# A buffer of their own and an earlier issue for the adaLN weight parts, with three raw weight buffers in place of four

## The chip, the core and the metric

One core of a Trainium2 chip runs the whole network in one launch. The metric is the device time of one execution in microseconds (us). Lower is better.

## The reference

The network maps a sequence of 256 tokens of width 1024 (fp32) to one of the same shape. It has two blocks:

- The first block has four layers. Each is a gated FFN, an attention (differential, MoBA, NSA, differential again) and a second gated FFN, each with an RMS norm ahead and a residual sum behind.
- The second block has two layers. Each is a mixer (retention and causal pooling) and a gated FFN, and both are modulated by adaLN: shifts, scales and gates are computed from a vector c.

An FFN has 2816 hidden columns:

```python
def swiglu(x, w_in, w_out):
    gate, up = jnp.split(x @ w_in, 2, axis=-1)
    return (jax.nn.silu(gate) * up) @ w_out
```

The modulation of the second block is a product of one row with a matrix of 1024 x 6144 for each of the two layers:

```python
for l in range(DEPTH_2):
    mod = c_act @ w_ada[l] + b_ada[l]
    sh1, sc1, g1, sh2, sc2, g2 = jnp.split(mod, N_MOD, axis=-1)
    h = modulate(rmsnorm(x, norm1[l]), sh1, sc1)
    ...
    x = x + g1[:, None, :] * (merged @ w_out[l])
    h2 = modulate(rmsnorm(x, norm2[l]), sh2, sc2)
    gate, up = jnp.split(h2 @ w_ffn_in[l], 2, axis=-1)
    x = x + g2[:, None, :] * ((jax.nn.silu(gate) * up) @ w_ffn_out[l])
```

The modulation does not depend on x, so it can be computed at any time before the second block needs it.

## The kernel before

**Stages.** The network is cut into 16 stages. Stages 0, 2, 3, 5, 6, 8, 9 and 11 are the FFNs of the first block, and 1, 4, 7 and 10 its attentions. Stages 12 and 14 are the mixers of the second block and 13 and 15 its FFNs. Each stage opens a memory pool `mp` of its own, and an attention or mixer stage also `ap`. A pool `wp` for weights lives through the whole program.

**Weights.** Every weight is loaded from HBM in pieces of 1 MB into a buffer with the tag `raw` in `wp`. There are four of them (RAW_BUFS = 4): loads in `weights` (L182) and, for some pieces of `seven`, L447. ScalarE casts a piece in halves of 1024 columns to a high part (`hilo`, L171, into `hi`), VectorE subtracts it for the low part (L172, into `lo`). There are seven buffers of either kind (W_BUFS = 7). TensorE multiplies high by high, low by high and high by low (L220, L222 and L224). Once both halves are split, the raw buffer is free.

**An FFN** has 11 chunks of 256 hidden columns for each of two halves of the tokens. `f1` makes the first product of a chunk; `hidden` applies the gate on ScalarE (L414) and VectorE (L416, L417), whose result `hd` is transposed to `hT`; `f2` multiplies it with w_out and sums in PSUM (`aA`, `aB`). PLAN cuts the middle of the FFN into two units. A unit has two plain chunks and one pair of chunks that is computed with seven block products in place of eight (`seven`). Its operands are sums of quarters of w_in, made by transfers that accumulate (POOL, L452) into tiles `rs`, and sums and differences of quarters of x, which `halves_of_x` makes once in each FFN. It uses one raw buffer as scratch (tag `raw`), and writes the results `Sh` and `Sl` (L171 and L172).

**The order of the work** in a unit is a string, `"fo777fo7fo7fo7ooo7no"` (L542): f is a first product, o a second product, 7 a step of `seven`, n starts the next unit's loads. After its places 9 and 15 `ada_step` is called, in all stages but the first. The framework then schedules the instructions onto each engine's queue ahead of time, by program order and by when it thinks that operands are ready, and each engine runs its queue in order. Buffers with the same tag are handed out in program order.

**adaLN parts.** The scales and shifts of the second block are computed in the FFNs of stages 2, 3, 5, 6, 8, 9, 11 and 13, one vector of 1024 for each FFN, in four parts (u = 0 to 3). `ada_add` (L1173) loads 1 MB of w_ada into a raw buffer (SP, L1179) and adds its rows, scaled by c, to an accumulator with four VectorE instructions (L1185 or L1187). After the fourth part `ada_columns` sums over the partitions with two small products. Stage 15 has no `ada_step` work left, and stage 0 has none. The two gates of each second-block layer are computed the same way, by `start_gate` in stages 12 to 15: four parts, with `yield GATE_STEP` ahead of each `ada_add`.

Of the kernel before, what the change touches and what calls it, by code (L numbers as in the profile page):

```python
# [18 lines left out]
P = 128  # L19
D = 1024  # L20
# [13 lines left out]
POOL_WINDOWS = (2, 4, 8, 16)  # L34
UW = 1024

RAW_BUFS = 4
W_BUFS = 7
PREP_0 = 4.4
PREP_1 = 0.6  # L40
# [62 lines left out]
class _Net:  # L103
# [70 lines left out]
    def weights(self, srcs, a, b):  # L174


        raw = self.t(self.wp, [P, 2 * UW], "raw", bufs=RAW_BUFS)
        rv = raw[:, : a * b].rearrange("p (a b) -> p a b", a=a)
# [221 lines left out]
    def ffn(self, w_in, w_out, factors, finish, middle, scaled):  # L400


        nc = self.nc
        hT, wi, wo, acc = {}, {}, {}, {}
# [29 lines left out]
        def seven(c):  # L434
# [7 lines left out]
            def load(k, n, alone=False):  # L442
                if alone:
                    r = self.t(self.wp, [P, 2 * UW], "raw", bufs=RAW_BUFS).rearrange("p (a b) -> p a b", a=4)
                else:
# [73 lines left out]
            yield  # L519

        queue, sums = [], {}

        def pop():
            c, t = queue.pop(0)
            f2(c, t=t)

        first = ((0, 0), (0, 1), (1, 0), (1, 1)) if self.stage == 0 else ((0, 0), (1, 0), (0, 1), (1, 1))
# [40 lines left out]
    def halves_of_x(self, res, scaled):  # L568
# [15 lines left out]

        f = self.t(self.wp, [P, 2 * UW], "raw", bufs=RAW_BUFS).rearrange("p (a b) -> p a b", a=4)
        x = {}
# [267 lines left out]
    def compress(self, k2, w1, pe):  # L854
# [11 lines left out]
        for u in range(2):  # L866
            raw = self.t(self.wp, [P, 2 * UW], "raw", bufs=RAW_BUFS)
            rv = raw.rearrange("p (a b) -> p a b", a=8)
# [301 lines left out]
        self.oner = self.t(self.cp, [P, P], "oner", F32R)  # L1170
        nc.vector.tensor_scalar(self.oner, self.ident, 0.0, 1.0, op0=ALU.mult, op1=ALU.add)

    def ada_add(self, acc, l, i, u, first=False):  # L1173

        nc = self.nc
        src = self.cols(self.a["w_ada_2"][l], i * D, D, 2 * u, 2)
        raw = self.t(self.wp, [P, 2 * UW], "raw", bufs=RAW_BUFS)
        rv = raw.rearrange("p (a b) -> p a b", a=2)
        nc.sync.dma_start(rv, src)  # L1179
        for k in range(2):  # L1180
            c = self.ccol[:, 2 * u + k : 2 * u + k + 1]
            for q in range(2):
                r = slice(512 * q, 512 * q + 512)
                if first and k == 0:
                    nc.vector.tensor_scalar(acc[:, r], rv[:, k, r], c, None, op0=ALU.mult)  # L1185
                else:
                    nc.vector.scalar_tensor_tensor(acc[:, r], rv[:, k, r], c, acc[:, r], op0=ALU.mult, op1=ALU.add)  # L1187
# [16 lines left out]
    def ada_step(self):  # L1204

        if not self.ada_steps:
            return
        l, i, u = self.ada_steps.pop(0)
        if u == 0:
            self.ada_acc = self.t(self.mp, [P, D], "ada", bufs=1)  # L1210
        self.ada_add(self.ada_acc, l, i, u, u == 0)
        if u == 3:
            self.start(self.ada_columns(self.ada_acc, l, i))

    def ada_columns(self, acc, l, i):
        nc = self.nc
        o = (l * 6 + i) * KT
        m = self.mod[:, o : o + KT]
        sums = yield from self.over_partitions(acc)
        for q, ps in enumerate(sums):  # L1220
            tmp = self.t(self.fp, [P, 4, P], "res", bufs=2)
            nc.vector.tensor_tensor(tmp, ps.rearrange("p (a b) -> p a b", a=4),
                                    self.ident[:, None, :].to_broadcast([P, 4, P]), op=ALU.mult)
            nc.vector.reduce_sum(m[:, 4 * q : 4 * q + 4], tmp, axis=AX.X)
        nc.vector.tensor_tensor(m, m, self.bcol[:, o : o + KT], op=ALU.add)
# [4 lines left out]
    def start_gate(self, l, i):  # L1230


        nc = self.nc
        g = self.t(self.fp, [P, D], "gbc", bufs=1)
        self.gate_done = False

        def gen():
            yield 4.0
            nc.gpsimd.memset(g, 0.0)
            nc.gpsimd.dma_start(g[0:1], self.a["b_ada_2"][l : l + 1, i * D : i * D + D])  # L1240
            for u in range(4):
                yield GATE_STEP
                self.ada_add(g, l, i, u)
            yield 4.0
            sums = yield from self.over_partitions(g)
            for q, ps in enumerate(sums):
                nc.scalar.activation(g[:, 512 * q : 512 * q + 512], ps, AF.Copy, scale=0.5)
            self.gate_done = True

        self.start(gen())  # L1250
        return g
# [362 lines left out]
```

## Time and profile before

| | us |
|---|---|
| median of 3 runs | 2959.21 |
| lowest and highest | 2957.91 and 2966.21 |
| profiled execution, its own time | 2968.85 |
| its span, first to last instruction | 2967.1 |
| TensorE (PE) busy | 2849.1 (96%) |
| VectorE (DVE) busy | 2177.2 (73%) |
| ScalarE (ACT) busy | 1679.8 (57%) |
| GpSimd (POOL) busy | 432.9 (15%) |
| TensorE's mean granted clock | 0.989 |

The rows that the prediction reads come from one profiled execution. PE is TensorE's matmuls and PEld its weight loads. DVE is VectorE, ACT is ScalarE, SP is the engine whose queue issues most transfers. A row `B <- A: x, n, y` of a list of waits says that B was held up by A for x us in total, n times, y us at the longest. In a timeline, a bracket `[x <-A]` at the end of a row means that the engine stood idle for x us before this instruction and that A ended the idle time. A timeline row with `xN` joins N equal neighbours; its duration covers them all. The granted clock 1.00 is 2.4 GHz, 0.50 is 1.2 GHz.

### The profile page before, as it was taken

To read this page: it belongs to the slowest core of one execution; us is meant where nothing else is said; L and a number is where in the kernel's file an instruction comes from. 1 tells how busy PE (TensorE), PEld (TensorE's weight loads), DVE (VectorE), ACT (ScalarE), POOL (GpSimd) and SP (SyncE) were. 2 spreads that over 40 slices of the span, in tenths; PEclk is the share of its full clock that TensorE was granted. 3 is DMA by queue.
4 is the path that set the end of the run, shared out by engine and by line. 5 is a ranking of instruction groups with operands and counts; after the bars stand their busy time and mean duration, and the time that the engine had idled before them with its cause. 6 is when DMAs were issued, how large, how long until landed. Compare 5 with 4: busy or idle time off the path is not lost.

```text
span 2967.1 us, 36810 instructions
## 1 busy us (share of the span) xinstructions
PE 2849.1 (96%) x13165; PEld 2274.3 (77%) x13165; DVE 2177.2 (73%) x3275; ACT 1679.8 (57%) x2873; POOL 432.9 (15%) x601
## 2 busy tenths in 40 slices
PE   8999999999999999999999999999999999999998
PEld 6787777777777777778777777777778777788777
DVE  7665778877467787756777877677876688865776
ACT  6556655655665565556655555665554454644554
POOL 1112211111111021121111111211111101100110
PEclk9999999999999999999999999999999999999999
DMA  9864497796449779751698795459764679664694
GB/s 274 233 198 158 136 306 225 216 273 213 149 141 291 226 225 259 218 190 44 185 267 250 233 264 184 142 179 262 233 226 172 191 235 297 226 220 163 213 274 147
DMA packets 358043, 633.27 MB, mean 213 GB/s; under 512 B 15170, under 2 KB 190132, under 8 KB 357860
## 3 DMA queue, kind: packets, MB, share of 16 engines
q1 hardware_dynamic: 312724, 541.99, 53.7%
q0 software_dynamic: 44768, 88.30, 16.2%
q8 instruction: 104, 1.70, 0.2%
q14 instruction: 79, 0.65, 0.1%
q10 hardware_dynamic: 368, 0.62, 0.1%
HBM read 629.82 MB, written 1.05 MB: 213 GB/s over the span
## 4 chain that ended last, share of the span: by engine, by line
PE 68%; DVE 13%; DMA 8%; ACT 5%; issue 4%; POOL 2%; DVEq 0%; SPq 0%; ACTq 0%; POOLq 0%
PE mm L222 13%; PE mm L224 13%; PE mm L220 13%; DMA raw<-in_w_ada_dram 6%; DVE lo L172 5%; PE tp L252 4%; PE aA L222 4%; PE aA L224 4%; PE aA L220 4%; ACT hi L171 3%; PE aB L222 3%; PE aB L220 3%; PE aB L224 3%; DVE Sl L172 1%; DVE ada L1187 1%
## 5 line engine op out<-in xcount | busy, mean ns | idle before, releaser
L172 DVE TENSOR_TENSOR lo<-raw,hi 128x1024 fp32r<-128x1024 f32 x834 | 1005.2, 1222 | 294.0 <-ACT hi L171 286.9
L171 ACT CAST hi<-raw 128x1024 fp32r<-128x1024 f32 x834 | 865.9, 1051 | 371.3 <-PE mm L224 176.6
L220 PE MATMUL mm<-hi,xh 128*128 128x512 f32 (+2 forms) x1856 | 750.8, 406 | 39.6 <-DVE hd L417 33.0
L222 PE MATMUL mm<-lo,xh 128*128 128x512 f32 (+2 forms) x1856 | 735.7, 397 | 4.8 <-DVE lo L172 4.8
L224 PE MATMUL mm<-hi,xl 128*128 128x512 f32 (+2 forms) x1856 | 732.1, 395 | 2.4 <-DVE xl L172 1.4
L220 PEld LDWEIGHTS mm<-hi,xh 128*128 128x128 f32 x1856 | 352.6, 190 | 123.7 <-issue 31.6
L224 PEld LDWEIGHTS mm<-hi,xl 128*128 128x128 f32 x1856 | 353.2, 190 | 80.0 <-DVE xl L355 4.8
L222 PEld LDWEIGHTS mm<-lo,xh 128*128 128x128 f32 x1856 | 353.9, 191 | 78.1 <-DVE lo L172 14.7
L452 POOL DMA_DIRECT2D rs<-in_ffn_w_in_dram x128 | 157.2, 1300 | 1104.1 <-DVE lo L172 785.5
L171 ACT CAST hi<-rs 128x1024 fp32r<-128x1024 f32 x200 | 205.8, 1049 | 167.1 <-PE mm L224 155.4
L172 DVE TENSOR_TENSOR lo<-rs,hi 128x1024 fp32r<-128x1024 f32 x200 | 239.6, 1221 | 42.7 <-ACT hi L171 41.8
L222 PE MATMUL mm<-lo,Sh 128*128 128x512 f32 x560 | 227.2, 406 | 7.7 <-DVE lo L172 7.3
L220 PE MATMUL mm<-hi,Sh 128*128 128x512 f32 x560 | 226.8, 405 | 4.0 <-ACT hi L171 4.0
L224 PE MATMUL mm<-hi,Sl 128*128 128x512 f32 x560 | 221.2, 395 | 0.0
L220 PE MATMUL aB<-hi,hT 128*128 128x512 f32 x568 | 195.1, 402 | 10.4 <-ACT hT L264 10.4
L220 PE MATMUL aA<-hi,hT 128*128 128x512 f32 x584 | 198.9, 404 | 0.9 <-DVE s L661 0.9
L224 PE MATMUL aB<-hi,hT 128*128 128x512 f32 x568 | 192.2, 392 | 0.9 <-DVE hT L268 0.8
L222 PE MATMUL aA<-lo,hT 128*128 128x512 f32 x584 | 192.3, 392 | 0.0
L224 PE MATMUL aA<-hi,hT 128*128 128x512 f32 x584 | 191.8, 392 | 0.0
L222 PE MATMUL aB<-lo,hT 128*128 128x512 f32 x568 | 189.4, 393 | 0.0
L264 ACT CAST hT<-tp 128x256 fp32r<-128x256 f32 x268 | 94.7, 372 | 161.7 <-PE tp L252 161.5
L265 DVE TENSOR_TENSOR hT<-tp,hT 128x256 fp32r<-128x256 f32 x268 | 108.5, 420 | 68.2 <-ACT hT L264 67.7
(281 smaller groups left out, 3670.7 us busy)
## 6 DMA issues: line engine op xcount, KB each, us to landing
raw<-in_ffn_w_in_dram SPq DMA_DIRECT2D x224, 512.0 KB, 7.2
raw<-in_ffn_w_out_dram SPq DMA_DIRECT2D x88, 1024.0 KB, 5.7
rs<-in_ffn_w_in_dram POOLq DMA_DIRECT2D x128, 512.0 KB, 8.9
raw<-in_w_ada_dram SPq DMA_DIRECT2D x48, 1024.0 KB, 6.8
raw<-in_w_in_dram SPq DMA_DIRECT2D x44, 1024.0 KB, 5.2
rs<-in_ffn_w_in_dram SPq DMA_DIRECT2D x32, 1024.0 KB, 6.7
raw<-in_ffn_w_in_dram SPq DMA_DIRECT2D x32, 1024.0 KB, 8.6
raw<-in_w_ffn_in_dram SPq DMA_DIRECT2D x56, 512.0 KB, 5.1
```

Of the source, the lines that this page charges most:

```text
L171: self.nc.scalar.copy(hi, raw)
L172: self.nc.vector.tensor_tensor(lo, raw, hi.bitcast(F32), op=ALU.subtract)
L220: mm(ps, xh[k], wh[:, c], start=first, stop=False)
L222: mm(ps, xh[k], wl[:, c], start=False, stop=False)
L224: mm(ps, xl[k], wh[:, c], start=False, stop=last)
L252: self.nc.tensor.transpose(dst, src, self.ident[:k, :k])
L264: nc.scalar.copy(hi, v)
L265: nc.vector.tensor_tensor(lo, v, hi.bitcast(F32), op=ALU.subtract)
L452: nc.gpsimd.dma_start(r[:, 2 * q : 2 * q + 2], quarter(k, n)[:, 2 * q : 2 * q + 2], accum_op=ALU.add)
L1187: nc.vector.scalar_tensor_tensor(acc[:, r], rv[:, k, r], c, acc[:, r], op0=ALU.mult, op1=ALU.add)
```

## The change

- `ada_load` is split off from `ada_add`. In an FFN stage it loads a part into a tile `araw` in the stage's own pool `mp` (one buffer of the size of a raw one); in a mixer stage, into a raw buffer as before.
- `ffn` issues the load of part 0 at its start. `ada_step` adds the part that was loaded before and then issues the load of the next part, if the FFN has one more.
- In `start_gate` the load of a part stands ahead of `yield GATE_STEP` rather than behind it.
- RAW_BUFS is 3 in place of 4.

```diff
-RAW_BUFS = 4
+RAW_BUFS = 3
...
         queue, sums = [], {}
+        if self.stage > 0 and self.ada_steps:
+            self.ada_next = self.ada_load(*self.ada_steps[0])
...
-    def ada_add(self, acc, l, i, u, first=False):
-
-        nc = self.nc
+    def ada_load(self, l, i, u):
+
         src = self.cols(self.a["w_ada_2"][l], i * D, D, 2 * u, 2)
-        raw = self.t(self.wp, [P, 2 * UW], "raw", bufs=RAW_BUFS)
+        if self.stages[self.stage]["attention"]:
+            raw = self.t(self.wp, [P, 2 * UW], "raw", bufs=RAW_BUFS)
+        else:
+            raw = self.t(self.mp, [P, 2 * UW], "araw", bufs=1)
         rv = raw.rearrange("p (a b) -> p a b", a=2)
-        nc.sync.dma_start(rv, src)
+        self.nc.sync.dma_start(rv, src)
+        return rv
+
+    def ada_add(self, acc, rv, u, first=False):
+
+        nc = self.nc
...
-        self.ada_add(self.ada_acc, l, i, u, u == 0)
+        self.ada_add(self.ada_acc, self.ada_next, u, u == 0)
         if u == 3:
             self.start(self.ada_columns(self.ada_acc, l, i))
+        else:
+            self.ada_next = self.ada_load(*self.ada_steps[0])
...
             for u in range(4):
+                rv = self.ada_load(l, i, u)
                 yield GATE_STEP
-                self.ada_add(g, l, i, u)
+                self.ada_add(g, rv, u)
```

## Rows read from the trace of the kernel before

**Rows 1.** The page: busy time, share of the span and instructions of each engine.
```profile
PE 2849.1 (96%) x13165; PEld 2274.3 (77%) x13165; DVE 2177.2 (73%) x3275; ACT 1679.8 (57%) x2873; POOL 432.9 (15%) x601
```
**Rows 2.** The page: the chain that ended last, by engine and line.
```profile
PE mm L222 13%; PE mm L224 13%; PE mm L220 13%; DMA raw<-in_w_ada_dram 6%; DVE lo L172 5%; PE tp L252 4%; PE aA L222 4%; PE aA L224 4%; PE aA L220 4%; ACT hi L171 3%; PE aB L222 3%; PE aB L220 3%; PE aB L224 3%; DVE Sl L172 1%; DVE ada L1187 1%
```
**Rows 3.** Waits of TensorE: total us, times, longest us.
```profile
PE mm L220 <- DVE hd L417: 33.0, 18, 4.3
```
**Rows 4.** Timeline of SP in stage 2: start us, us, queue, line, operation.
```profile
384.90 0.37 SPq L1179 DMA_DIRECT2D raw<-in_w_ada_dram  x1
...
395.89 0.37 SPq L1179 DMA_DIRECT2D raw<-in_w_ada_dram  x1
...
401.54 9.21 SPq L182 DMA_DIRECT2D raw<-in_ffn_w_in_dram  x4
```
**Rows 5.** Timeline of VectorE in the same stretch of stage 2.
```profile
390.85 0.48 DVE L1185 TENSOR_SCALAR ada<-raw,col 128x512 f32<-128x512 f32 x1
...
406.73 2.08 DVE L1187 SCALAR_TENSOR_TENSOR ada<-raw,col,ada 128x512 f32<-128x512 f32 x3 [4.09 <-DMA raw<-in_w_ada_dram]
...
409.72 0.47 DVE L417 SCALAR_TENSOR_TENSOR hd<-hd,fs,mm 128x256 f32<-128x256 f32 x1
```
**Rows 6.** Timeline of TensorE behind it.
```profile
410.34 0.47 PE L220 MATMUL mm<-hi,xh 128*128 128x512 f32 x1 [3.26 <-DVE hd L417]
```
**Rows 7.** Windows, first unit: stretch, us, busy us; then PEclk, DMA share, GB/s.
```profile
67.80:91.40 23.60, 23.60 (x106) 18.95 (x105) 16.56 (x22) 13.20 (x18) 4.86 (x5) 1.00 1.05 256
2816.60:2840.20 23.60, 23.60 (x106) 18.94 (x105) 16.22 (x21) 12.84 (x17) 4.93 (x5) 1.00 1.03 251
...
1107.70:1137.70 30.00, 25.72 (x105) 20.48 (x104) 21.03 (x29) 13.16 (x18) 4.90 (x5) 0.89 1.07 286
...
sum 229.00, PE 203.28 PEld 161.56 DVE 168.13 ACT 104.82 POOL 39.19; mean PE 25.41 PEld 20.19 DVE 21.02 ACT 13.10 POOL 4.90
```
**Rows 8.** Windows, second unit, sum of its eight stretches.
```profile
sum 198.00, PE 191.93 PEld 151.66 DVE 173.92 ACT 103.82 POOL 39.17; mean PE 23.99 PEld 18.96 DVE 21.74 ACT 12.98 POOL 4.90
```
**Rows 9.** Windows of 3.4 us right after the gap of rows 6.
```profile
411.20:414.60 3.40, 3.40 (x11) 2.61 (x10) 1.13 (x2) 1.32 (x2) 1.20 (x1) 0.50 1.09 369
415.00:418.40 3.40, 3.40 (x16) 2.81 (x15) 2.29 (x4) 2.45 (x3) 0.00 (x0) 1.00 1.05 226
```
**Rows 10.** Window of stage 3's start.
```profile
543.00:573.00 30.00, 28.16 (x132) 22.37 (x131) 29.04 (x50) 18.89 (x37) 2.05 (x5) 1.00 0.59 186
```
**Rows 11.** The loads of line 1179: who waited for them, and issue to landing.
```profile
  DVE ada L1187: 50.7, 16
...
DMA to landing us min/median/max: 5.0/6.8/11.7
```
**Rows 12.** Waits of SP's queue: total us, times, longest us.
```profile
SPq L182 <- DVE lo L172: 1425.1, 260, 17.1
...
SPq L447 <- DVE on L1098: 45.8, 1, 45.8
```
**Rows 13.** Waits of all engines.
```profile
ACT hi L171 <- PE mm L224: 333.3, 305, 6.1
```
**Rows 14.** Timeline of SP at the start of stage 3.
```profile
551.39 0.37 SPq L182 DMA_DIRECT2D raw<-in_ffn_w_out_dram  x1
565.82 1.89 SPq L447 DMA_DIRECT2D raw<-in_ffn_w_in_dram  x2
569.61 3.55 SPq L182 DMA_DIRECT2D raw<-in_ffn_w_in_dram  x4
```
**Rows 15.** Timeline of ScalarE at the start of stage 3.
```profile
571.27 1.05 ACT L171 CAST hi<-raw 128x1024 fp32r<-128x1024 f32 x1 [3.75 <-DMA raw<-in_ffn_w_in_dram]
```
**Rows 16.** Timeline of TensorE at the start of stage 3.
```profile
562.35 0.71 PE L220 MATMUL aA<-hi,hT 128*128 128x512 f32 x2
...
571.35 0.62 PE L222 MATMUL aA<-lo,hT 128*128 128x512 f32 x2
...
573.63 0.40 PE L220 MATMUL mm<-hi,Sh 128*128 128x512 f32 x1
```

More of the change, by code (lines that the diff above doesn't have):

```diff
@@ L1171, in ada_setup @@
         nc.vector.tensor_scalar(self.oner, self.ident, 0.0, 1.0, op0=ALU.mult, op1=ALU.add)
-    def ada_add(self, acc, l, i, u, first=False):
+    def ada_load(self, l, i, u):
+        src = self.cols(self.a["w_ada_2"][l], i * D, D, 2 * u, 2)
+        if self.stages[self.stage]["attention"]:
+            raw = self.t(self.wp, [P, 2 * UW], "raw", bufs=RAW_BUFS)
+        else:
+            raw = self.t(self.mp, [P, 2 * UW], "araw", bufs=1)
+        rv = raw.rearrange("p (a b) -> p a b", a=2)
+        self.nc.sync.dma_start(rv, src)
+        return rv
+    def ada_add(self, acc, rv, u, first=False):
         nc = self.nc
-        src = self.cols(self.a["w_ada_2"][l], i * D, D, 2 * u, 2)
-        raw = self.t(self.wp, [P, 2 * UW], "raw", bufs=RAW_BUFS)
-        rv = raw.rearrange("p (a b) -> p a b", a=2)
-        nc.sync.dma_start(rv, src)
         for k in range(2):
```

## Prediction

> **What bounds the kernel.** I began with the page's busy times: TensorE is busy 2849.1 of 2967.1 us, VectorE 73% [rows 1]. A change off TensorE can pay only through TensorE's idle time, about 118 us, or through its clock. Then the chain of waits: it puts 6% on the w_ada transfers [rows 2]. That is no ceiling: the chain counts a transfer from its issue, while TensorE still has work. The waits of TensorE are the better measure: the largest single entry is 33.0 us in 18 waits for L417, the product that finishes a hidden chunk [rows 3].
>
> The timelines of stage 2 (the second FFN) show how w_ada causes it. SP issues part 0 at 384.90 and part 1 at 395.89, and from 401.54 four w_in transfers follow [rows 4]. VectorE runs its queue in order. It begins part 0 at 390.85, about as soon as a 5 us transfer can have landed; the adds are evidently placed at the moment the schedule thinks their data is there. For part 1 this is too early: VectorE stands still for 4.09 us until 406.73, and L417, which is queued behind, runs at 409.72 [rows 5]. TensorE waits 3.26 us for it [rows 6].
>
> The same piece of work, from the third plain chunk's first product on, some 105 matmuls, stands in stages 0 and 15 without adaLN parts: 23.60 us. In the eight FFNs with parts it takes 229.0 us together, against 8 x 23.6 = 188.8: 40.2 us too long; in the worst, 30.0 us, the granted clock is 0.89 [rows 7]. In the second unit, where parts 2 and 3 lie, the eight take 198.0 us: 9.2 us too long [rows 8]. So **the change can win 49 us at most**. Part of it is the clock: right after the gap of stage 2, 3.4 us hold 11 matmuls at a granted clock of 0.50 (1.2 GHz), the next 3.4 us 16 at 1.00 (2.4 GHz) [rows 9], so such a stretch costs 5/16 x 3.4 = 1.1 us.
>
> **Part by part.** *Own buffer and early issue.* No byte, transfer or add goes; 32 parts in FFNs are re-timed, and 16 gate parts, half of them in the second block's FFNs and so through the new buffer. Part 0 is issued at the FFN's start and cannot be late. Part k+1 can start only when the last of part k's four adds has read the single buffer; before, it could take another of four. A load then waits on SP for VectorE, with the weight loads behind it. Seven hi/lo buffers cover that while VectorE is only a few us late; without the cover such a wait delays weights by its length. I take nothing, up to 4 us in each FFN. In stage 2 part 1's load would now come after the adds of part 0, which VectorE, full at the FFN's start (29.04 of 30 us in stage 3 [rows 10]), reaches some 10 us before it did. So part 1 comes into the quiet time in which part 0 landed, and part 2 possibly into the crowd in which part 1 was late.
>
> A part lands 5.0 to 11.7 us after issue, median 6.8, and VectorE waits 50.7 us in 16 of 32 cases for these [rows 11]: two of four parts late in each FFN. After the change I reckon with one. Its price is from 1.15 us (9.2/8, the second unit's excess) to 5.0 us (40.2/8, the first unit's); I take 2.2, nearer to the lower end because in the second unit, where most late parts cost little, the same wait of VectorE falls where fewer products are queued behind. Gain: 49.4 - 8 x 2.2 = **32 us**; bounds 49 (none late) and 4 (as late as before, with only the second unit's half won back). Adds that are pulled into the full 30 us at an FFN's start could cost up to 2.8 us there (three of the four took 2.08 [rows 5]); they stand later in program order than the work there, so I take nothing.
>
> *Three raw buffers.* Where the stretch is steady this is hidden: loads wait for a slot anyway (1425.1 us in 260 waits of SP on the low half's subtraction [rows 12]), because the casts behind them wait for TensorE to free a hi buffer (333.3 us in 305 waits [rows 13]); I take 4 us in sum for attention, NSA's compression and mixers (where the gate now holds a slot one step longer); bounds 0 and 10.
>
> It is not hidden at an FFN's start. There `halves_of_x` holds a raw buffer as scratch for its sums and differences. In stage 3 four slots let w_out's first load go at 551.39; two loads L447 follow at 565.82, when the scratch is done, and four w_in from 569.61 [rows 14]. Slots are handed out in program order, so with three w_out gets the slot of 565.82, and each L447 load the slot after, about 1.9 us (the span of the pair) later. L447's first cast comes 5.45 us after its issue and ScalarE stood 3.75 us for that transfer [rows 15]. So w_out would be cast at about 571.3 + 1.05, with the low half at 573.5; TensorE used it at 562.35, a few matmuls, and at 571.35 in a block of ten; the first product with Sh, fed by L447, came at 573.63 [rows 16]. The block of ten is late by 1 to 2 us. L447 is late by the slot (1.9 us) and possibly by w_out's megabyte in front of it (5.45 us more), 7.3 in all; the two delays overlap, and the products of other w_in chunks can fill some of it. Bounds per start: 0, if these fill all, and 7.3 + 1.1 (clock). I take 2.2, next to the slot's delay, since the DMA engines have room there for both transfers at once. Eight first-block FFNs: 17.6, and 2 x 1.5 = 3 in the second block's, whose two starts I did not follow singly. Together **21 us**.
>
> The DMA engines are 0.59 busy there [rows 10], so part 0's megabyte fits in the 12 us left; without that cover it adds one issue and one transfer, up to 5 us, in front of a weight. A load into a new stage's pool can also wait on SP for the stage before, as L447 did once for 45.8 us [rows 12]; that load stands there already, so I take nothing more.
>
> Two rules bear on this. The row on landing shows that the same megabyte takes 5.0 or 11.7 us. The Trainium skill, page *DMA: Bandwidth & Descriptors*, section "Issuing engines are not separate DMA queues", says that transfers from different engines' queues interleave on the same 16 engines. The trace agrees (a share of 1.07 in the worst stretch [rows 7]); by that rule an early issue alone shortens no transfer, and the sum would lose most of its gain: rival 2 below.
>
> The gap repeats in eight FFNs at the same place. The Trainium skill, page *Perfetto Trace Analysis*, section "Optimization Strategy", says that consistent bubbles can mean too little room for the next tile, buffer counts included. By that rule a fourth raw buffer is the last thing to give up, and the sum would be that of rival 3. No row of this kernel shows three buffers.
>
> **Sum:** -32 + 21 + 4 = -7 us. The profiled execution took 2968.85 us (span 2967.1), 9.64 above the median 2959.21, and no row tells why; I take the terms from it and put the sum to the median: **2952 us**. About 0.3%, 9 us, is what can be told from no change.
>
> **Rivals.**
> 1. *The gap goes whole.* Parts 1 to 3 find quiet times, and TensorE fills FFN starts with other products. For it: stages 0 and 15 run the stretch at 23.60 us. 49 less 4 for what is left, and starts at 1.0 each (10) give -35: 2924 us.
> 2. *The wait only moves.* Each load is issued when the buffer is free and its add placed as soon as the schedule believes it landed. For it: the 0.75 us between earliest landing and 390.85; against: part 0 is surely early. Gain 4 to 10, starts 15, others 4: about 2970 us.
> 3. *Slower: the scratch's slot decides.* L447 and w_out come so late at every FFN's start that TensorE stands and falls to its lower clock. Per start 5.0 idle (nearly the one transfer's 5.45) and 1.1 clock: 10 x 6.1 = 61, others 4, less the gain of 32, is +33: 2992 us. It decides from about 4 us per start on, where starts and the 4 us outweigh the gain by over 9. For it: ScalarE already stands 3.75 us for L447 there; against: 0.59 of the DMA engines, and other chunks' products ready.
>
> **Chances.** Forecast 0.36, its own range 2938 to 2966 (14 us either way, the gain and the starts together); rival 1: 0.27; rival 2: 0.15; rival 3: 0.22. Faster by over 0.3% (below 2950) takes rival 1 and 0.13 of the forecast: 0.40. Slower (above 2968) takes rival 3, 0.09 of rival 2 and 0.01 of the forecast: 0.32. Same: 0.28. The range of 8 in 10 leaves out about 0.1 at each end, the better part of rival 1 and the worse half of rival 3: 2920 to 2988.
>
> **What would show it.** Right: VectorE's waits for w_ada fall from 50.7 us to about 20; TensorE's wait for L417 from 33.0 to about 15; the first unit's stretch is near 25 us; and new gaps of 1 to 3 us stand before w_out's first block or the first product with Sh in each FFN, with w_out issued at the scratch's release. Wrong towards rival 1: no new gaps there. Towards rival 2: waits for w_ada as long as now, elsewhere. Towards rival 3: gaps of 4 us and more at FFN starts with a granted clock of 0.5 behind. A new wait of SP for the buffer with late casts behind it would break the step that I cost at nothing, and so would adds inside the full 30 us.

## The result and the profile after

The changed kernel takes 3044.43 us (median of four, 3038.06 to 3051.96), the kernel before 2958.74 beside it: a ratio of 1.0285, with a 95% interval of 1.0255 to 1.0314. It is 85.7 us slower. The profiled execution of the changed kernel took 3042.66 us, 1.8 below its median; that of the kernel before lies 10.1 above its own, so the two spans differ by less than the medians.

The page of the changed kernel, its span and busy times (they answer to [rows 1]):

```profile
span 3040.9 us, 36791 instructions
...
PE 2865.3 (94%) x13165; PEld 2287.6 (75%) x13165; DVE 2179.2 (72%) x3275; ACT 1685.8 (55%) x2873; POOL 433.4 (14%) x601
```

The span grew by 73.8 us. TensorE has the same 13165 matmuls, but is busy 16.2 us longer, at a mean granted clock of 0.979 in place of 0.989, and idle 57.6 us longer (175.6 against 118.0). The waits of TensorE say where (they answer to [rows 3]):

```profile
PE tp L252 <- DVE sc L485: 64.6, 16, 7.8
PE mm L222 <- DVE lo L172: 32.2, 28, 3.6
...
PE mm L220 <- DVE hd L417: 12.8, 8, 2.8
```

The wait for L417, which the change was to take away, did fall, from 33.0 to 12.8 us. In its place stands one for L485, which multiplies the gate and the other half of a Strassen pair before it is transposed: 64.6 us. The wait for a low half of weights (L172), 12.1 us in the kernel before, is 32.2.

**The wait for L485.** The timeline of SP in stage 2 after the change (beside [rows 4]):

```profile
385.41 0.37 SPq L1183 DMA_DIRECT2D araw<-in_w_ada_dram  x1
...
407.02 0.92 SPq L182 DMA_DIRECT2D raw<-in_ffn_w_in_dram  x2
410.48 0.37 SPq L1183 DMA_DIRECT2D araw<-in_w_ada_dram  x1
```

and of VectorE (beside [rows 5]):

```profile
415.43 1.23 DVE L172 TENSOR_TENSOR lo<-rs,hi 128x1024 fp32r<-128x1024 f32 x1 [3.58 <-ACT hi L171]
422.08 0.75 DVE L1196 SCALAR_TENSOR_TENSOR ada<-araw,col,ada 128x512 f32<-128x512 f32 x1 [5.42 <-DMA araw<-in_w_ada_dram]
...
427.69 0.69 DVE L485 SCALAR_TENSOR_TENSOR sc<-res,sc 128x512 f32<-128x512 f32 x1
```

and of TensorE (beside [rows 6]):

```profile
428.43 1.11 PE L252 MATMUL tp<-cst,sc 128*128 128x128 f32 x4 [5.01 <-DVE sc L485]
```

Part 2 is issued at 410.48, when VectorE has read part 1 out of the single buffer, and is there at 422.08, 11.6 us later, behind two w_in transfers and among the accumulating ones. One of its four adds is placed on VectorE at 416.7, so VectorE stands still for 5.42 us, and then has low halves, sums and L485 to do before TensorE can go on. The clock falls behind the gap. The windows of 3.4 us from its end, and 1.2 us further on:

```profile
428.40:431.80 3.40, 3.37 (x10) 2.89 (x11) 3.30 (x5) 0.89 (x2) 0.01 (x1) 0.50 0.83 293
433.00:436.40 3.40, 3.40 (x17) 2.76 (x16) 2.74 (x4) 2.10 (x2) 1.24 (x1) 1.00 1.09 280
```

A gap like this, of 4.4 to 7.8 us, stands once in each first-block FFN with parts, twice in stage 13 (for a gate's part and for an adaLN part) and once in stage 15 (a gate's part). The loads of the parts in the changed kernel, who waits for them and how long they take (beside [rows 11]):

```profile
  DVE ada L1196: 55.7, 12
  DVE gbc L1196: 22.8, 5
  DVE ada L1194: 2.2, 2
...
DMA to landing us min/median/max: 5.1/7.4/15.5
```

**The FFN's start.** SP in stage 3 (beside [rows 14]; the stage runs about 12 us later than before, the first step of `halves_of_x` begins at 560.94 in place of 549.07):

```profile
557.42 7.74 SPq L182 DMA_DIRECT2D raw<-in_ffn_w_in_dram  x4
576.37 0.37 SPq L182 DMA_DIRECT2D raw<-in_ffn_w_out_dram  x1
579.37 2.64 SPq L447 DMA_DIRECT2D raw<-in_ffn_w_in_dram  x2
```

TensorE there after the change (beside [rows 16]):

```profile
577.87 0.50 PE L222 MATMUL mm<-lo,xh 128*128 128x512 f32 x1 [3.38 <-DVE lo L172]
```

The cast of that piece of w_in on ScalarE, with the one after it, and the low half that VectorE makes for it:

```profile
565.81 2.24 ACT L171 CAST hi<-raw 128x1024 fp32r<-128x1024 f32 x2
576.60 1.21 DVE L172 TENSOR_TENSOR lo<-raw,hi 128x1024 fp32r<-128x1024 f32 x1
```

The same low half in the kernel before, and what TensorE did just ahead of it there:

```profile
563.96 1.23 DVE L172 TENSOR_TENSOR lo<-raw,hi 128x1024 fp32r<-128x1024 f32 x1
564.64 0.73 PE L220 MATMUL aB<-hi,hT 128*128 128x512 f32 x2 [1.58 <-ACT hT L264]
```

And ScalarE's first cast of w_out after the change (beside [rows 15], where it was L447 that came late):

```profile
581.40 1.05 ACT L171 CAST hi<-raw 128x1024 fp32r<-128x1024 f32 x1 [5.66 <-DMA raw<-in_ffn_w_out_dram]
```

Against the stage's own start, w_out goes 13 us later (576.37 - 551.39 - 11.9), as late as the scratch is held, and L447 1.7 us later; both were foreseen. TensorE stands 3.38 us, and its row names a low half of w_in, which VectorE makes at 576.60 behind the chain of `Sl`. But that half is hardly later than it was. Its piece was loaded and cast by 568.1, and counted from the first step of `halves_of_x` the low half begins 15.7 us on, against 14.9 in the kernel before. What is gone is the work ahead of it: before, TensorE had two products with w_out at 562.35 [rows 16] and two at 564.64, and came to the low half when it was ready. After the change the first product with w_out comes at 583.36. So TensorE stands in the hole that the late w_out leaves.

**By stage.** The time from the first instruction that makes a stage's low part of x to that of the next stage, from the traces (the last column is the sum of the seven first-block FFNs with parts, 2, 3, 5, 6, 8, 9 and 11):

| kernel | stage 2 | stage 3 | stage 13 | stage 15 | seven FFNs |
|---|---|---|---|---|---|
| before | 198.7 | 194.9 | 197.1 | 200.2 | 1390.2 |
| changed | 208.4 | 201.9 | 215.5 | 211.1 | 1433.4 |

Of the 73.8 us, 43.2 lie in the seven FFNs, 18.4 in stage 13 and 10.9 in stage 15. Attentions and mixers are as they were (966.6 and 966.9 us together).

### The profile page after: what moved, and what is told of

The parts are those of the page before. It is cut to its first block, busy times and chain, and to the rows that moved or that the text cites. A ratio compares the mean times of both kernels' runs of the same rounds, so it can differ in the third digit from the quotient of the medians.

```text
span 3040.9 us, 36791 instructions
## 1 busy us (share of the span) xinstructions
PE 2865.3 (94%) x13165; PEld 2287.6 (75%) x13165; DVE 2179.2 (72%) x3275; ACT 1685.8 (55%) x2873; POOL 433.4 (14%) x601
## 2 busy tenths in 40 slices
DMA packets 358043, 633.27 MB, mean 208 GB/s; under 512 B 15170, under 2 KB 190132, under 8 KB 357860
## 5 line engine op out<-in xcount | busy, mean ns | idle before, releaser
L172 DVE TENSOR_TENSOR lo<-raw,hi 128x1024 fp32r<-128x1024 f32 x834 | 1006.0, 1220 | 286.0 <-ACT hi L171 276.1
L220 PE MATMUL mm<-hi,xh 128*128 128x512 f32 (+2 forms) x1856 | 748.3, 405 | 20.1 <-DVE hd L417 12.8
L222 PE MATMUL mm<-lo,xh 128*128 128x512 f32 (+2 forms) x1856 | 734.2, 396 | 24.9 <-DVE lo L172 24.9
L222 PEld LDWEIGHTS mm<-lo,xh 128*128 128x128 f32 x1856 | 353.9, 191 | 95.7 <-DVE lo L172 31.3
L172 DVE TENSOR_TENSOR lo<-rs,hi 128x1024 fp32r<-128x1024 f32 x200 | 240.5, 1220 | 74.6 <-ACT hi L171 72.8
L222 PE MATMUL mm<-lo,Sh 128*128 128x512 f32 x560 | 231.0, 412 | 7.5 <-DVE lo L172 7.4
L222 PE MATMUL aB<-lo,hT 128*128 128x512 f32 x568 | 196.2, 405 | 0.0
L222 PE MATMUL aA<-lo,hT 128*128 128x512 f32 x584 | 193.6, 392 | 0.0
```

Of the source, the lines that this page charges most:

```text
L172: self.nc.vector.tensor_tensor(lo, raw, hi.bitcast(F32), op=ALU.subtract)
L220: mm(ps, xh[k], wh[:, c], start=first, stop=False)
L222: mm(ps, xh[k], wl[:, c], start=False, stop=False)
```

## The experiments

Two theories at first. **A**: the single buffer and the order of the adds make the loss (the wait ahead of L485). **B**: the third raw buffer makes it. Each ratio below is to the kernel before on the same chip in the same rounds, and "us over" is the difference of these medians.

**One part of the change alone.** *raw3*: the kernel before with three raw buffers.

```diff
-RAW_BUFS = 4
+RAW_BUFS = 3
```

> The kernel before with three raw buffers and nothing else. Theory A (the single adaLN buffer makes each load follow the adds of the part before, the third load falls into the crowd of the other transfers, and VectorE stands 5 to 8 us for it with L485 behind it) gives most of the 85 us to the buffer and the order: here only the FFN starts get worse, by 2 to 3 us each, 2975 to 2990 us, TensorE's wait for L417 stays near 33 us and none for L485 appears. Theory B (the missing raw buffer is the cause, everything else follows from late weights) gives 3030 to 3045 us here.

3033.77 us, 1.0241 (1.0215 to 1.0268), 71.6 us over. That is within B's range and 44 us above A's. The waits of TensorE in this run:

```profile
PE mm L222 <- DVE lo L172: 75.3, 54, 3.6
PE tp L252 <- DVE sc L485: 23.3, 9, 3.8
```

The late weights are the larger part here and the L485 wait the smaller, the reverse of the changed kernel. So two kernels of nearly the same time lose it in different places.

*order4*: the changed kernel with the adds of parts 1 to 3 held in program order on VectorE in the first block.

```diff
+                if acc is self.ada_acc and u > 0 and self.stage < 12:
+                    self.tc.keep_in_program_order(ins)
```

> The changed kernel, with the adds of parts 1 to 3 in the first-block FFNs kept on VectorE behind everything that stands ahead of them in program order, so that they can't be issued early and wait. Theory A: the wait for L485 goes in the seven first-block FFNs (it stays in the two of the second block), some 7 x 6 us idle and some 10 us of low clock: 2980 to 3000 us. Theory B: 3035 to 3045 us, with the gap only in another place.

2992.08 us, 1.0096 (1.0077 to 1.0115), 29.9 us over: A's figure. The four adds of part 1 now run in one piece, without a wait, and TensorE's wait for L485 falls from 64.6 us in 16 to 22.8 in 3, those of stages 13 and 15. VectorE of this run in stage 2:

```profile
429.22 2.73 DVE L1196 SCALAR_TENSOR_TENSOR ada<-araw,col,ada 128x512 f32<-128x512 f32 x4
```

and TensorE's waits:

```profile
PE mm L222 <- DVE lo L172: 34.0, 28, 4.5
PE tp L252 <- DVE sc L485: 22.8, 3, 7.8
```

So 55.8 us (85.7 - 29.9) of the changed kernel are VectorE's early adds in the first block, and both theories hold a part. In the traces order4 takes 1385.7 us in the seven FFNs, 47.7 less than the changed kernel and about what they took before the change. What is left of the loss lies in stages 13 (217.6) and 15 (210.6), where no add was held.

**What the parts and the third buffer cost each by itself.** *none4* is the kernel before and *none3b* the same with three buffers, both without the 32 parts; *none3* is the changed kernel without them. They leave that part of the computation out; the gates' 16 parts stay in all three. The edit, in none3 with its early loads gone as well:

```diff
-        self.ada_add(self.ada_acc, l, i, u, u == 0)
+        if u == 0:
+            self.nc.vector.memset(self.ada_acc, 0.0)
```

> The changed kernel without the loads and adds of the 32 adaLN parts in FFNs (the accumulator is set to zero; the gates' parts stay). It leaves out that part of the computation. Theory A: without parts three raw buffers cost 20 to 30 us at FFN starts against the 49 us that the parts cost before: 2930 to 2950 us. Theory B: three buffers cost their 85 us here as well, less the parts' own: 2990 to 3010 us.

> The kernel before without the loads and adds of the 32 adaLN parts in FFNs (the accumulator is set to zero). It leaves out that part of the computation. Theory A (at an FFN's start the scratch of halves_of_x holds one of the three raw buffers, and w_out's first load waits for it; this costs about 3 us in each FFN, with or without parts): 2910 to 2925 us, some 45 below the same with three buffers (2968.68 was measured). Theory B (three buffers cost little without parts, it is the parts that need the fourth): 2945 to 2965 us.

> The kernel before with three raw buffers and without the 32 adaLN parts in FFNs (left out, the accumulator set to zero); the gates' parts as before, through the raw buffers. Measured so far: 2916.65 with four raw buffers, 2968.68 with three and the gates through the single FFN buffer. If the third buffer alone costs the 52 us, 2960 to 2970; if the gates' way through the single buffer in the two FFNs of the second block is 20 us of it, 2940 to 2952.

- none4: 2916.65 us, 0.9850 (0.9835 to 0.9864), 45.9 us under the kernel before.
- none3b: 2963.18 us, 1.0013 (1.0001 to 1.0026), 4.4 over.
- none3: 2968.68 us, 1.0022 (1.0012 to 1.0031), 6.5 over.

The parts cost the kernel before 45.9 us. The third buffer costs **50.3 us without the 32 parts**, twice the 25 us that the forecast gave it. None3 lies between the two theories' figures; in the expectations from none4 on, A stands for the scratch as the cause, and none4 alone is where A put it. The gates' way through the single buffer adds 2.1, less than the noise of these medians. By stage none4 to none3b is 1346.5 to 1373.4 us in the seven FFNs, 8.7 in stage 13 and 7.4 in stage 15. TensorE's waits, first in none4:

```profile
PE mm L222 <- DVE lo L172: 13.8, 26, 1.6
```

then in none3b:

```profile
PE mm L222 <- DVE lo L172: 38.6, 31, 3.9
PE tp L252 <- DVE sc L485: 13.1, 9, 2.1
...
PE aA L220 <- ACT hi L171: 6.5, 2, 3.7
```

These three rows of none3b are nearly the whole price, by place. For each FFN I compared when TensorE has begun the same share of the stage's matmuls in the two traces, counted from the stage's start; they differ by 42.7 us in all.

- **The start**, 19.7 us. After a third of the matmuls none3b is behind by 2.1 to 2.9 us in eight of the nine FFNs (0.8 in stage 11). This is the gap ahead of L222, 3.0 to 3.9 us in each of the seven, with no product of w_out before it, as in stage 3 above. Stage 0 loses nothing.
- **The second unit's pair**, 13.6 us more by six tenths, in each of the nine. Its first L447 load is issued 7.4 to 9.8 us later against the stage's start than in none4. ScalarE stands 1.5 to 2.9 us for it, as it does nowhere there in none4, and L485 is queued on VectorE behind the low half. In stage 2:

```profile
440.44 1.05 ACT L171 CAST hi<-raw 128x1024 fp32r<-128x1024 f32 x1 [2.92 <-DMA raw<-in_ffn_w_in_dram]
441.52 1.23 DVE L172 TENSOR_TENSOR lo<-raw,hi 128x1024 fp32r<-128x1024 f32 x1 [2.59 <-ACT hi L171]
442.67 0.69 DVE L485 SCALAR_TENSOR_TENSOR sc<-sc,sc 128x512 f32<-128x512 f32 x1
```

- **w_out in stages 13 and 15**, 9.6 us more by seven tenths. ScalarE stands 5.0 and 4.0 us for a load of w_out, and TensorE 3.7 and 2.7 us behind it. The gates' parts take raw buffers in these two stages; that they are what delays w_out was not tested.

**Is it the scratch?** *none3_scr* is none3, and *raw3_scr* is raw3, with the scratch in a buffer of the FFN's own:

```diff
-        f = self.t(self.wp, [P, 2 * UW], "raw", bufs=RAW_BUFS).rearrange("p (a b) -> p a b", a=4)
+        f = self.t(self.mp, [P, 2 * UW], "araw", bufs=1).rearrange("p (a b) -> p a b", a=4)
```

> Three raw buffers, no adaLN parts in FFNs (left out as in none3), and the scratch of halves_of_x in the FFN's own buffer in place of a raw one. Theory A: the gaps of 3 to 4 us ahead of L222 at the FFN starts go, 2925 to 2940 us. Theory C (it is the three buffers in the units, where the loads of the Strassen pair and w_out come close together, that cost): 2955 to 2970 us, start gaps gone or not.

> The kernel before with three raw buffers, the scratch of halves_of_x in an FFN buffer of its own, the parts in the raw buffers as before. 3033.77 us was measured with the scratch in a raw buffer. Theory A: about 35 us are won back, 2995 to 3005 us, and what is left over 2959 is the parts' place among three buffers. Theory C: less than 15 us, 3018 to 3034.

none3_scr: 2960.80 us, 0.9995 (0.9985 to 1.0006), 8.3 less over than none3. raw3_scr: 3013.02 us, 1.0183 (1.0165 to 1.0201), 21.1 less over than raw3. In none3_scr the wait for low halves falls from 38.6 to 21.1 us, but that for L485 rises from 27.6 to 32.4. Compared with none4 as above, the lag at the start of the seven FFNs falls from 15.5 us in none3 to 7.7, and what comes after it only from 15.8 to 13.2. In stages 13 and 15 of none3_scr the scratch shares its one buffer with the gates' loads, and nothing is won there. The scratch at the FFN's start is a part of the price, not the most of it, without parts and with them; theory C in the expectations is right without parts, and raw3_scr lies between the two figures, nearer to C's.

**Undoing the rest.** *gate_undone*: the gates' loads behind the yield again, in raw buffers.

```diff
-                rv = self.ada_load(l, i, u)
                 yield GATE_STEP
-                self.ada_add(g, rv, u)
+                self.ada_add(g, self.ada_load(l, i, u, False), u)
```

> The changed kernel with the gates' part of the change undone in the FFNs of the second block: each load behind the yield, into a raw buffer (of three). If the single buffer, with the gates in its chain, makes the 29 us that the second block's two FFNs lost, 3015 to 3025 us and the gaps of 7 to 8 us ahead of the transposes of sc go there; if it is the third raw buffer, 3038 to 3048 and the gaps are there, in another form.

3032.63 us, 1.0253 (1.0234 to 1.0272), 73.9 over: 11.8 us are from the gates' part of the change, and the time lies between the two figures. Stage 13 takes 210.7 us in place of 215.5, stage 15 207.5 in place of 211.1.

*own_late*: the single buffer without the early issue, each part loaded at its own step.

```diff
-        if self.stage > 0 and self.ada_steps:
-            self.ada_next = self.ada_load(*self.ada_steps[0])
...
-        self.ada_add(self.ada_acc, self.ada_next, u, u == 0)
+        self.ada_add(self.ada_acc, self.ada_load(l, i, u), u, u == 0)
```

> The changed kernel without the early issue in ada_step: three raw buffers, a part in its own buffer, loaded at its own step right ahead of its adds (the gates as changed). If the early issue is what makes a third load follow the second part's adds into the crowd, the L485 gaps go in the seven first-block FFNs and the L417 gaps of the kernel before come back, 3005 to 3025 us. If early issue is worth what it was meant to, this is slower than 3044.

3044.51 us, 1.0292 (1.0273 to 1.0312), 85.7 over: the time of the changed kernel. The expectation failed: the L485 gaps do not go.

```profile
PE tp L252 <- DVE sc L485: 65.4, 14, 10.3
```

With the single buffer the place in the program at which a load is asked for makes no difference in the time. The schedule issues it in either case about when the buffer is free: in stage 2 the parts go at 338.6, 381.8, 405.8 and 442.1 us here, and at 333.8, 385.4, 410.5 and 444.9 in the changed kernel. What own_late alone shows, VectorE standing 3.5 to 3.8 us for part 0 at the start of stages 3, 6 and 9, leaves no mark on the seven FFNs together (1434.0 us).

*early4*: the early issue with four raw buffers and no own one.

```diff
-RAW_BUFS = 3
+RAW_BUFS = 4
...
-        if self.stages[self.stage]["attention"]:
-            raw = self.t(self.wp, [P, 2 * UW], "raw", bufs=RAW_BUFS)
-        else:
-            raw = self.t(self.mp, [P, 2 * UW], "araw", bufs=1)
+        raw = self.t(self.wp, [P, 2 * UW], "raw", bufs=RAW_BUFS)
```

> The early issue alone: four raw buffers, and the parts in them as before, each issued one step ahead. Theory A: a load need no longer follow the adds of the part before, so the 5 to 8 us waits ahead of L485 go, but a part holds a raw buffer from step to step: 2955 to 2990 us. Theory B: weights have three buffers for most of an FFN, as in the changed kernel: 3030 to 3045 us.

2954.87 us, 0.9970 (0.9957 to 0.9983): 7.3 us *under* the kernel before, at the lower end of A's range. The L485 wait is 3.7 us in 2, the one for L417 24.9. What the change was to bring is there in this form, if little of it.

**The adds in order, four raw buffers.** *f_order* keeps every add in program order on VectorE, *f_order2* only those of the 32 parts, not the gates'; nothing else differs from the kernel before.

```diff
-                    nc.vector.scalar_tensor_tensor(acc[:, r], rv[:, k, r], c, acc[:, r], op0=ALU.mult, op1=ALU.add)
+                    ins = nc.vector.scalar_tensor_tensor(acc[:, r], rv[:, k, r], c, acc[:, r], op0=ALU.mult, op1=ALU.add)
+                if acc is self.ada_acc:
+                    self.tc.keep_in_program_order(ins)
```

This is f_order2's edit, without the same change to the line of the first add; f_order has it without the `if`.

> The kernel before, four raw buffers, with every adaLN add kept on VectorE behind what stands ahead of it in program order. If the waits of VectorE for parts that the schedule takes as landed are what the kernel before loses (the 49 us over the stretches without parts), 2915 to 2940 us, and TensorE's wait for L417 falls from 33 to under 10 us. If the adds, once in the queue at a fixed place, wait as long there or delay other work, 2955 to 2975 us.

> The kernel before, four raw buffers, with only the 32 adaLN parts' adds kept in program order on VectorE, not the gates'. 2938.00 us was measured with the gates in order too, where the two FFNs of the second block took 5 and 7 us more than before. If these are from the gates, 2925 to 2933 us; if the parts in the first FFN of the second block make them, 2934 to 2940.

f_order: 2938.00 us, 0.9924 (0.9907 to 0.9941). f_order2: **2925.29 us, 0.9893 (0.9871 to 0.9914)**, 33.5 us under the kernel before, and faster than either kernel of this study. The gates' adds in order cost the difference: stages 13 and 15 take 202.0 and 207.1 us in f_order, 193.4 and 199.2 in f_order2. The page and TensorE's waits of f_order2:

```profile
span 2918.1 us, 36817 instructions
...
PE 2828.0 (97%) x13165; PEld 2255.4 (77%) x13165; DVE 2177.0 (75%) x3275; ACT 1677.5 (57%) x2873; POOL 430.8 (15%) x601
```
```profile
PE tp L252 <- ACT res L1273: 12.4, 8, 2.6
PE mm L222 <- DVE lo L172: 11.6, 23, 1.6
```

The wait for L417 is down to 3.1 us in 3, and the granted clock is 0.998. VectorE does the four adds of part 1 of stage 2 in one piece from 419.50, some 17 us after the part landed (issued at 391.8, 11.1 us on the way), and no wait of TensorE follows:

```profile
419.50 2.73 DVE L1187 SCALAR_TENSOR_TENSOR ada<-raw,col,ada 128x512 f32<-128x512 f32 x4
```

**Order and buffers together.** *raw3_order* is f_order2 with three raw buffers, *early4_order* early4 with the parts' adds in order (both by the lines already shown).

> The kernel before with three raw buffers and with the adaLN parts' adds kept in program order on VectorE. With four buffers parts in order cost 12 us over no parts (ratios 0.9893 and 0.9850 to the kernel before). If the early adds are what made three buffers worse with parts (1.0241) than without (1.0013), 2970 to 2980 us; if the parts need the fourth buffer for themselves, 3000 to 3020.

> Four raw buffers, each part issued one step ahead into a raw buffer, the parts' adds kept in program order on VectorE. Against 2925.29 us for the same order without early issue: if the early issue gains once the adds wait their turn, 2915 to 2922 us; if it only holds a raw buffer longer, 2930 to 2955.

raw3_order: 3006.81 us, 1.0162 (1.0139 to 1.0184), 45.0 over. early4_order: 2988.45 us, 1.0093 (1.0078 to 1.0108), 26.6 over. raw3_order lies in its second range, that the parts need the fourth buffer for themselves; early4_order is slower than either of its two. With the adds in order the third buffer costs 78.4 us (from 33.5 under to 45.0 over), more than the 50.3 without parts. The early issue then costs 60.1 (from 33.5 under to 26.6 over). A raw buffer that a part holds longer, until its adds' turn or from step to step, would explain both, and the wait for low halves fits it (11.6 us in f_order2, 33.0 in early4_order); no run isolates it. TensorE's first wait in raw3_order is again that for weights:

```profile
PE mm L222 <- DVE lo L172: 55.6, 42, 3.6
```

## Why the prediction was wrong

2952 us was forecast, 2920 to 2988, and 3044.43 measured. The runs take the 85.7 us apart in four terms. In each the first figure is that of the kernel before and the second that of the changed one.

| term | before | changed | difference | runs |
|---|---|---|---|---|
| raw buffers, without parts | 0 | 50.3 | 50.3 | none4, none3b |
| gates through the single buffer | 0 | 2.1 | 2.1 | none3b, none3 |
| parts, adds in order | 12.4 | 23.4 | 11.0 | none4, f_order2; none3, order4 |
| adds placed before their data | 33.5 | 55.8 | 22.3 | f_order2, before; order4, changed |

They add up by construction, since each is a step between neighbouring runs. The terms are not independent: gate_undone shows that with parts the gates weigh 11.8 rather than 2.1, and taken first, with parts and early adds as before, the third buffer costs 71.6 (raw3) and the rest of the change 14.1. Nor are the last two rows quite alike on both sides: f_order2 holds the adds of all 32 parts, order4 those of parts 1 to 3 in the first block alone. By the traces most of the third row's difference lies in stage 13, whose adds order4 leaves early (217.6 us, 204.7 in none3). In the seven FFNs ordered parts cost 8.9 (none3 to order4) against 6.8 (none4 to f_order2).

- **What could be won** was right. Two stages without parts gave 49 us; none4 measured 45.9. That the early adds are the cause was right too: holding them back wins 33.5 us with nothing else changed.
- **The step on the own buffer failed by its price.** "After the change I reckon with one. Its price is from 1.15 us ... to 5.0 us." One part waited for at length in each FFN is what came, and TensorE's wait for L417 fell to 12.8 us where about 15 was forecast. But VectorE's waits for parts did not fall to 20 us: they are 55.7 us in 12 in place of 50.7 in 16, fewer and longer. And a late part costs 6.8 us (order4 saves 47.7 us in the traces of the seven FFNs), beyond the upper bound. I took the bound from stretches of the kernel before in which VectorE waited 5.1 us at most. A load that can start only when the buffer has been read lands later against the place of its adds: VectorE waits up to 8.3 us, with L485 behind it, and the clock falls after. The text named that chain ("part 2 possibly into the crowd") and then priced it by rows in which it did not occur.
- **The step on the early issue was wrong in kind.** Own_late, without it, has the same time. With one buffer, where the program asks for a load was no lever; with four raw buffers it won 7.3 us (early4).
- **The step on three raw buffers was the largest error, and it failed in the units.** 21 us for the FFN starts and 4 us for attentions and mixers were taken; 50.3 were measured, 42.7 between the traces. The starts were read rightly: the scratch holds the slot, w_out goes 13 us late, and TensorE stands where it had w_out's first few products. They lost 19.7 us, 2.2 on average in nine, and stage 0, which was priced too, nothing. Attentions and mixers lost 1.1. What failed is "Where the stretch is steady this is hidden", under which the units of the FFNs stood at nothing. They lost 23.2 us, 13.6 at the second unit's pair and 9.6 at w_out in stages 13 and 15. Waits of SP for a slot show that loads queue, not that a slot fewer is free of charge. The casts' wait for a hi buffer was counted as cover for that; none3b shows that it is not enough.
- **The rivals.** The mechanism of rival 2, the wait that only moves, is what order4 shows. It was to give back the gain and make 2970 us; it gave back the gain and 22.3 us more, and it did not come alone. Rival 3 looked for its loss at the FFN's start, at 6.1 us each; 2.2 came, and the rest lay in the units. Neither had both at once, and the range reached only to one of them.

The Trainium skill, page *Perfetto Trace Analysis*, section "Optimization Strategy", says that a bubble which repeats can mean too few buffers. The runs agree: with one raw buffer fewer and nothing else, a gap of 3.0 to 3.9 us stands at the start of each of the seven FFNs, and 50.3 us in all. The page's rule was named in the prediction and its rival given 0.22.

Two things stay open. The loads in the units that lack the fourth raw buffer are read from the traces of none4 and none3b; no run gives a buffer back to one of them alone. And the own buffer beside *four* raw ones was not tried.

## What to carry to other kernels

An engine that runs its queue in order can pay for an instruction that is placed before its data: look for rows in which it stands for a transfer with urgent work behind, and hold such filler work in program order before giving it memory; here that one line wins 1.1%. A buffer that loads queue for is not spare because they queue anyway: take one away alone, with nothing else changed, and time it, before trading it. An early issue was worth nothing here through a single buffer whose reader is late.

## What was not expected of the hardware

- The clock is a good part of it. From the kernel before to f_order2 TensorE is busy 21.1 us less (2849.1 to 2828.0) with the same 13165 matmuls, and the mean granted clock goes from 0.989 to 0.998: of the 49.0 us between the two spans these 21.1 are not idle time, but matmuls that run at 2.4 in place of 1.2 GHz. Busy time times clock is nearly the same in both, 2818 and 2822 us. The two profiled executions lie 10.1 us above and 5.4 below their medians, so the medians differ by less, 33.5 us.
- The same megabyte of w_ada took 5.1 to 15.5 us in the changed kernel (5.0 to 11.7 before), with the same transfers in all: 633.27 MB on both pages. What differs is when they are issued and what else is on its way; which of the other transfers made the long ones is not shown.
